# Value columns of two head pairs projected token-major in one group and convolved along tokens by shifted reads, in a gated-DeltaNet / mLSTM layer on Trainium2

## The chip, the cores and the metric

The kernel runs on one core of a Trainium2 chip. The metric is the device time of one execution in microseconds. The core has TensorE (PE in the profile; its weight loads are PEld), VectorE (DVE), ScalarE (ACT), GpSimd (POOL) and SyncE (SP), whose queue issues nearly all DMAs of this kernel.

## The reference

One decoder layer on 256 tokens of width 2048, with two branches, a gated DeltaNet (32 value heads in 16 pairs that share a query and a key head) and an mLSTM. All is float32. Cut to what matters here:

```python
h = rms_norm(x, norm_pre_w) * (1.0 + scale[:, None]) + shift[:, None]
proj = h @ w_in                                   # 16 groups of 512 columns for the pairs, and others
qkv = causal_conv_silu(gdn_qkv, gdn_conv_w)       # 4 taps along the tokens, per channel, then silu
q_a, k_a, v_a = jnp.split(qkv, [GDN_QK_WIDTH, 2 * GDN_QK_WIDTH], axis=-1)
q_a, k_a = l2_normalize(q_a) * 128 ** -0.5, l2_normalize(k_a)       # per head, shared by two value heads
o_a = gated_delta_rule(q_a, k_a, v_a, g_log, beta)                  # needs inverse of unit-lower matrices
o_a = rms_norm(o_a, gdn_norm_w) * silu(gdn_z)
y_a = o_a @ w_proj_gdn
# ... mLSTM branch gives y_b ...
merged = sigmoid(gate_a) * y_a + sigmoid(gate_b) * y_b
return x + gate * rms_norm(merged @ w_out, norm_post_w)
```

The convolution mixes a channel's value at token t with those at t-1, t-2 and t-3, each with its own weight per channel.

## The kernel before

**Precision.** Every large product takes float32 data as a rounded part and a remainder (`hi`, `lo`) and adds three products: hi·hi, hi·lo, lo·hi. Weights are split on the fly: a unit of weights (128x2048) is loaded by SP, and for each of its two pieces of 1024 columns ScalarE writes the rounded part (`whi`, line 173) and VectorE subtracts (`wlo`, line 177). Each has four buffers, the raw weights three. In the first part of the kernel, GpSimd does some of the subtractions.

**The stream.** `Stream.run` goes through all pieces in one order. It prepares up to four pieces ahead of the one that TensorE uses, issues the matmuls of a piece, then calls `side.step()`. A step so is one piece. All other work (convolutions, scores, block inverse, second stage, outputs) is written as generators that the `Side` object advances by one `yield` per step, in order of rank; `wait(n)` yields n times. `side.debt` is a planner's estimate of VectorE time that is booked and not yet worked off (1.6 us per step): the block inverse issues its next operation only when the debt leaves room.

**Two orientations.** `add_proj_t` projects channel-major: the weights are the stationary operand, the tokens (both halves of h side by side, 512 columns) move; per 128 rows of the contraction there are two matmuls of 512 columns (line 639) and two of 256 (line 643) for 256 output channels. `add_proj_n` projects token-major: h is stationary, 512 weight columns move, three matmuls of 512 columns for each block of 128 tokens (line 244). In both cases a piece is four such blocks.

**A period.** The DeltaNet runs in eight periods (`gdn_period(zg)`) of two head pairs. A pair's 512 columns are a query, a key and two value heads. Before the change a period is: channel-major pair 0 (8 pieces: first the half with query and key, then the half with two value heads), token-major output gate (`add_z`, 8 pieces), channel-major pair 1 (8 pieces), so 24 steps. For each half `conv_half` copies one part of the two sums on ScalarE (line 684), adds the other on VectorE (688), makes the first tap on ScalarE (691), three taps for each of two channel blocks on VectorE (697) and a Silu (705).

**Scores and values.** `gdn_stage1(p, ...)` forms the pair's score matrices (`psa`, `psb`, lines 761 to 766) when its convolutions are done, and transposes the four 128x128 blocks of values to token-major (`psv`, line 771), which ScalarE copies into `rr` scaled by the key norm (line 812). `block_rows` writes diagonal blocks of the scores to DRAM, `base_inverse` (after the second pair of the period) reads them back in another layout, inverts 32x32 blocks on VectorE, and writes and reads the result again (`ud`, `ug`, `xd`, `xcmp`). `gdn_stage2` starts at the earliest 31 steps after the second pair's scores; it puts the inverse together and applies it to `rr` (lines 960 to 989), then norms, gates and writes the heads to DRAM (`o_dr`).

**What sets the order.** Every engine executes its queue in program order, so an instruction that waits holds up those behind it; SP's queue holds weight loads and the transfers of the side work alike. The conv taps of the DeltaNet lie channel on partition in `gcv` (128x256, loaded by `late_consts`). Buffers of the pool `yp` (tags `ya`, `yhi`, `ylo`) serve `conv_half` here and the output projections later.

Of the kernel before, what the change touches and what calls it, by code (L numbers as in the profile page):

```python
# [7 lines left out]
F32 = mybir.dt.float32  # L8
F32R = mybir.dt.float32r
# [6 lines left out]
P = 128  # L16
# [102 lines left out]
def hybrid_layer_kernel(  # L119
# [153 lines left out]
    gate_row_dr = dr.tile([1, D], F32, name="gate_row_dr")  # L273
    START = [40 + g for g in range(8)] + [33, 37, 34, 38, 35, 39]
# [260 lines left out]
    def gates(ps):  # L535
# [52 lines left out]
        SP.dma_start(rows[32:40], mm_[64:72])  # L588
        yield from wait(3)
# [6 lines left out]
        V.tensor_scalar(ngt, tt[:, :, 0:32], -1.0, None, op0=ALU.mult)  # L596

# [28 lines left out]
    def add_proj_t(g, first, after, extra=None):  # L626

        w = w_in[g].rearrange("p (k n) -> p k n", k=KC)
        st_ = {}
        for hf in range(2):  # L630
            for t in range(2):
# [20 lines left out]
                stream.add(w[:, t * 8:(t + 1) * 8, hf * S:(hf + 1) * S], prep_w, use, after=done if t else None)  # L652
# [3 lines left out]
    def add_proj_n(g, after, extra=None):  # L656

        st_ = {}
        for t in range(4):
# [9 lines left out]
            stream.add(w_in[g][:, t * 2048:(t + 1) * 2048], prep_w, use, after=  # L669
# [4 lines left out]
    def conv_half(ps, taps, dst, hf, add=1, late=0, home=0, whole=False):  # L674
# [4 lines left out]
        elif home:  # L679
            ab = [bp.tile([P, S], F32, name="ab", tag=t, bufs=1) for t in ("p2", "tmp")]  # L680
        else:
            ab = [yp.tile([P, S], F32, name="ab", tag=("ya", ("yhi", "ylo")[i])[hf], bufs=3 - hf) for i in range(2)]
# [23 lines left out]

    def gdn_qk(ps, taps, qs, r, late):

        yield from conv_half(ps, taps, qs, 0, 1, late)
        qh = bp.tile([P, 2, S], F32R, name="qh", tag="qh", bufs=1)  # L710
        A.copy(qh, qs[:, 0:2])
        r.update(qh=qh)
# [29 lines left out]
    def gdn_taps(p):  # L742
        return lambda n, j: late_c["gcv"][:, (p * 4 + n) * 4 + j:(p * 4 + n) * 4 + j + 1]

    def gdn_stage1(p, ps, qs, pr, res):

        z = p % 2
        yield from conv_half(ps, gdn_taps(p), qs, 1, *((1, 0) if z else (3, 1)))
        qh = pr["qh"]
        side.debt += 0.7  # L750
        ql = bp.tile([P, 2, S], F32R, name="ql", tag="ql", bufs=1)
        V.tensor_tensor(ql, qs[:, 0:2], qh.bitcast(F32), op=ALU.subtract)
        yield
        gb = decay_rows(2 * p)
# [4 lines left out]
        yield from banks(3)  # L759
# [5 lines left out]
        for m in range(2):  # L765
            T.transpose(psb[:, 256 + m * P:256 + (m + 1) * P], qs[:, 0, m * P:(m + 1) * P], ident)
# [790 lines left out]
```

## Time and profile before

| | us |
|---|---|
| three runs: median (lowest to highest) | 1570.83 (1570.33 to 1573.07) |
| the profiled execution | 1570.67 |
| its span, first to last instruction | 1568.9 |
| mean granted TensorE clock | 0.998 |
| PE, DVE, ACT, POOL busy | 1555.8, 1166.0, 967.5, 261.5 |
| bytes moved by DMA | 372.22 MB, mean 237 GB/s |

The profile shows one execution. Busy times add up the time in which an engine had an instruction running. Matmuls are pipelined and their ends are modelled, so two neighbours overlap in the trace; how fast they follow one another is read from their starts. Rows of groups read: line, engine, operation, output and inputs, shapes, count | busy us, mean ns of one | idle time just before them and what ended it. Rows of the timeline read: start us, duration us, engine, line, operation, count of merged instructions. Rows of windows read: start:end, length, busy us and count for PE, PEld, DVE, ACT, POOL, then the granted clock, the share of DMA engines in use, and GB/s.

The eight periods lie between about 330 and 950 us; the mLSTM part, the output projections and the merge follow.

### The profile page before, as it was taken

To read this page: it belongs to the slowest core of one execution; us is meant where nothing else is said; L and a number is where in the kernel's file an instruction comes from. 1 tells how busy PE (TensorE), PEld (TensorE's weight loads), DVE (VectorE), ACT (ScalarE), POOL (GpSimd) and SP (SyncE) were. 2 spreads that over 40 slices of the span, in tenths; PEclk is the share of its full clock that TensorE was granted. 3 is DMA by queue.
4 is the path that set the end of the run, shared out by engine and by line. 5 is a ranking of instruction groups with operands and counts; after the bars stand their busy time and mean duration, and the time that the engine had idled before them with its cause. 6 is when DMAs were issued, how large, how long until landed. Compare 5 with 4: busy or idle time off the path is not lost.

```text
span 1568.9 us, 23204 instructions
## 1 busy us (share of the span) xinstructions
PE 1555.8 (99%) x8574; PEld 1308.5 (83%) x8574; DVE 1166.0 (74%) x1901; ACT 967.5 (62%) x1629; POOL 261.5 (17%) x212
## 2 busy tenths in 40 slices
PE   8999999999999999999999999999999999999997
PEld 5888888888888888888888888888888888888886
DVE  6785556765789898989898988776868866756654
ACT  7754446765666676767676777766566554544443
POOL 5787771000000010101010101000000000100100
PEclk9999999999999999999999999999999999999999
DMA  9998775975565656565656565657779877766573
GB/s 379 403 387 328 274 282 196 287 251 194 171 209 174 194 166 201 172 200 173 200 173 200 173 200 179 194 166 250 274 271 343 312 268 290 287 237 243 211 268 108
DMA packets 167739, 372.22 MB, mean 237 GB/s; under 512 B 26021, under 2 KB 127797, under 8 KB 140105
## 3 DMA queue, kind: packets, MB, share of 16 engines
q1 hardware_dynamic: 167240, 370.13, 68.2%
q8 instruction: 67, 1.10, 0.3%
q10 hardware_dynamic: 290, 0.53, 0.1%
q14 instruction: 46, 0.38, 0.1%
q0 software_dynamic: 96, 0.09, 0.0%
HBM read 354.40 MB, written 16.31 MB: 236 GB/s over the span
## 4 chain that ended last, share of the span: by engine, by line
PE 83%; issue 13%; DMA 2%; POOL 1%; ACT 1%; DVE 0%; SPq 0%; DVEq 0%; POOLq 0%; ACTq 0%
PE pn L244 38%; PE pt L639 19%; PE pt L643 9%; PE py L244 8%; POOL mg L1347 1%; DMA raw<-in_dram 1%; PE psa L244 1%; PE csil L314 0%; PE po L989 0%; PE po L988 0%; PE pc L978 0%; PE pb L968 0%; PE pa L960 0%; PE po L986 0%; PE pt L1028 0%
## 5 line engine op out<-in xcount | busy, mean ns | idle before, releaser
L177 DVE TENSOR_TENSOR wlo<-raw,whi 128x1024 fp32r<-128x1024 f32 (+1 forms) x455 | 558.8, 1236 | 221.6 <-ACT whi L173 220.5
L173 ACT CAST whi<-raw 128x1024 fp32r<-128x1024 f32 x508 | 523.9, 1046 | 269.4 <-PE pn L244 138.0
L244 PE MATMUL pn<-whi,h 128*128 128x512 f32 x1792 | 563.8, 392 | 1.2 <-ACT part L488 0.5
L639 PE MATMUL pt<-h,whi 128*128 128x512 f32 x1280 | 407.9, 400 | 0.0
L244 PEld LDWEIGHTS pn<-whi,h 128*128 128x128 f32 x1792 | 336.3, 188 | 72.3 <-ACT h L173 1.1
L244 PE MATMUL pn<-wlo,h 128*128 128x512 f32 x896 | 348.8, 389 | 0.0
L643 PEld LDWEIGHTS pt<-h,wlo 128*128 128x128 f32 x1280 | 240.4, 188 | 56.6
L643 PE MATMUL pt<-h,wlo 128*128 128x256 f32 x1280 | 251.9, 278 | 0.0
L639 PEld LDWEIGHTS pt<-h,whi 128*128 128x128 f32 x1280 | 195.5, 189 | 1.9
L244 PEld LDWEIGHTS pn<-wlo,h 128*128 128x128 f32 x896 | 168.3, 188 | 33.6
L177 POOL TENSOR_TENSOR wlo<-raw,whi 128x1024 fp32r<-128x1024 f32 (+1 forms) x67 | 146.5, 2199 | 47.3 <-ACT whi L173 41.6
L244 PE MATMUL py<-whi,yhi 128*128 128x512 f32 x384 | 150.6, 392 | 0.0
L244 PE MATMUL py<-whi,ylo 128*128 128x512 f32 x384 | 149.6, 390 | 0.0
L244 PE MATMUL py<-wlo,yhi 128*128 128x512 f32 x384 | 149.4, 389 | 0.0
L173 ACT CAST yhi<-ya 128x512 fp32r<-128x512 f32 x48 | 29.9, 623 | 127.6 <-PE py L244 124.3
L486 DVE TENSOR_TENSOR part<-pn,part 128x512 f32<-128x512 f32 x112 | 73.8, 686 | 45.1 <-PE pn L244 44.9
L730 POOL TENSOR_SCALAR_AFFINE_SELECT dd<-gb 128x256 f32<-128x256 f32 x40 | 33.9, 870 | 435.4 <-DMA gb<-rows 398.9
L177 DVE TENSOR_TENSOR ylo<-ya,yhi 128x512 fp32r<-128x512 f32 x48 | 33.2, 691 | 75.3 <-ACT yhi L173 71.8
L244 PEld LDWEIGHTS py<-whi,yhi 128*128 128x128 f32 x384 | 72.1, 188 | 15.3
L244 PEld LDWEIGHTS py<-whi,ylo 128*128 128x128 f32 x384 | 72.1, 188 | 15.1
L244 PEld LDWEIGHTS py<-wlo,yhi 128*128 128x128 f32 x384 | 72.1, 188 | 14.9
L697 DVE SCALAR_TENSOR_TENSOR qs<-ab,gcv,qs 128x255 f32<-128x255 f32 (+2 forms) x192 | 81.0, 477 | 0.0
(264 smaller groups left out, 1602.8 us busy)
## 6 DMA issues: line engine op xcount, KB each, us to landing
raw<-in_dram SPq DMA_DIRECT2D x259, 1024.0 KB
ar<-in_dram SPq DMA_DIRECT2D x31, 1024.0 KB
raw<-in_dram SPq DMA_DIRECT2D x16, 512.0 KB
ya<-o_dr SPq DMA_DIRECT2D x32, 256.0 KB
gate_dr<-part SPq DMA_DIRECT2D x11, 512.0 KB
gb<-rows SPq DMA_DIRECT2D x20, 256.0 KB
raw<-in_dram SPq DMA_DIRECT2D x6, 768.0 KB
ug<-ud SPq DMA_DIRECT2D x32, 128.0 KB
```

What stands on the lines that cost most here:

```text
L173: A.copy(hi, src)
L177: eng.tensor_tensor(lo, src, hi.bitcast(F32), op=ALU.subtract)
L244: T.matmul(ps, l, r, start=start and i == 0, stop=stop and i == 2, skip_group_check=True)
L486: V.tensor_tensor(part[g][:, b], ps[b], part[g][:, b], op=ALU.add)
L639: T.matmul(ps, hi[:, o:o + P], h2[:, k].rearrange("p a s -> p (a s)"), start=k == 0, stop=k == KC - 1, skip_group_check=True)
L643: T.matmul(ps[:, 0:S], lo[:, o:o + P], h_hi[:, k], start=False, stop=k == KC - 1, skip_group_check=True)
L697: V.scalar_tensor_tensor(dst[:, n, sh:], ab[i][:, 0:S - sh], taps(n, 3 - sh), dst[:, n, sh:], op0=ALU.mult, op1=ALU.add)
L730: G.affine_select(dd[:, :, blk * S:blk * S + P], gb[:, :, blk * P:(blk + 1) * P], pattern=[[0, 2], [1, P]], compare_op=ALU.is_ge, fill=-1e ...
L1347: G.tensor_tensor(mcols(b, hf, cg), mcols(b, hf, cg), s_, op=ALU.add)
```

## The change

A period becomes: query and key of both pairs channel-major (8 pieces: pair 0's, then pair 1's), the values of both pairs (4 heads, 512 columns) token-major in one group (8 pieces), the output gate (8 pieces). The transposes of values fall away, since the values come out token-major.

Token-major, the convolution runs along partitions. So `gdn_values` copies the sums to `rr`, waits 11 steps, writes them to a DRAM buffer `vd` (three rows of zeros stand ahead of the tokens), and reads them back shifted by one, two and three rows. The taps, now needed along the free dimension and equal on all partitions, are transposed once at the end of `gates`, written to `conv_dr` and read with a broadcast over 128 partitions in each period. GpSimd multiplies two of the shifted copies with their taps and adds them; VectorE does the other two and the remaining sums; ScalarE applies Silu and the key norm's scale. The second stage waits in its generator until `rr` is ready.

`gdn_stage1` convolves only query and key; both pairs share one tile `qs`. In `base_inverse` two waits become the same for all periods. `conv_half` takes its buffers from the tag `ylo` throughout, where it isn't in the late mLSTM pairs.

```diff
     def load_w(src):
-        for s_ in src if isinstance(src, tuple) else (src,):
+        for i, s_ in enumerate(src if isinstance(src, tuple) else (src,)):
+            if isinstance(src, tuple) and len(s_.shape) == 3:
+                SP.dma_start(raw.rearrange("p (k g c) -> p k g c", k=4, g=2)[:, :, i], s_)
+                continue
...
+    conv_dr = dr.tile([NPAIR, 4, 4, P], F32, name="conv_dr")
+    vd = dr.tile([S + 3, 512], F32, name="vd")
...
+        for z in range(2):
+            SP.dma_start(vd[0:3, z * S:(z + 1) * S], zz[0:3])
...
+        gct, gcp = t_("gct"), t_("gcp")
+        G.tensor_copy(gcp.rearrange("c (p t n) -> c p t n", n=4, t=4),
+                      late_c["gcv"].rearrange("c (p n t) -> c p t n", n=4, t=4))
+        yield from wait(2)
+        tc_ = gtile("tc")
+        for b in range(2):
+            T.transpose(tc_[:, b * P:(b + 1) * P], gcp[:, b * P:(b + 1) * P], ident)
+        A.copy(gct, tc_[:, 0:S])
+        yield from wait(2)
+        for b in range(2):
+            SP.dma_start(conv_dr[8 * b:8 * b + 8].rearrange("p t n c -> (p t n) c"), gct[:, b * P:(b + 1) * P])
...
     def add_proj_t(g, first, after, extra=None):
-        w = w_in[g].rearrange("p (k n) -> p k n", k=KC)
         for hf in range(2):
+            w = w_in[g[hf] if isinstance(g, tuple) else g].rearrange("p (k n) -> p k n", k=KC)
+            c0 = 0 if isinstance(g, tuple) else hf * S
...
     def add_proj_n(g, after, extra=None):
...
+            if isinstance(g, tuple):
+                src = tuple(w_in[i].rearrange("p (k n) -> p k n", k=KC)[:, 4 * t:4 * t + 4, S:2 * S] for i in g)
...
-    def gdn_stage1(p, ps, qs, pr, res):
+    def gdn_stage1(p, ps, qs, res):
         z = p % 2
-        yield from conv_half(ps, gdn_taps(p), qs, 1, *((1, 0) if z else (3, 1)))
-        qh = pr["qh"]
+        yield from conv_half(ps, gdn_taps(p // 2), qs, z)
+        qz = qs[:, 2 * z:2 * z + 2]
+        qh = bp.tile([P, 2, S], F32R, name="qh", tag="qh", bufs=1)
+        A.copy(qh, qz)
+        gb = decay_rows(2 * p)
+        yield from wait(1 + z)
         side.debt += 0.7
         ql = bp.tile([P, 2, S], F32R, name="ql", tag="ql", bufs=1)
...
-        psv = gtile("psv", True)
-        side.debt -= 1.6
-        for blk in range(2):
-            for h in range(2):
-                T.transpose(psv[:, (blk * 2 + h) * P:(blk * 2 + h + 1) * P],
-                            qs[:, 2 + h, blk * P:(blk + 1) * P], ident)
+        side.debt -= 1.2
...
-        for blk in range(2):
-            A.activation(res["rr"][:, blk, z], psv[:, blk * S:(blk + 1) * S], AF.Copy, scale=sk[:, blk:blk + 1])
-        gfree(psv)
+    def gdn_values(zg, ps, res):
+        rr = bp.tile([P, 2, 2, S], F32, name="rr", tag="rr")
+        for b in range(2):
+            A.copy(rr[:, b].rearrange("p z c -> p (z c)"), ps[b])
+        yield from wait(11)
+        SP.dma_start(vd[3:].rearrange("(b t) c -> t b c", b=2), rr.rearrange("p b z c -> p b (z c)"))
+
+        def tap_rows(w, z, j):
+            SP.dma_start(w, conv_dr[2 * zg + z, j:j + w.shape[1], 2:4].rearrange("t n c -> t (n c)").unsqueeze(0)
+                         .broadcast_to(list(w.shape)))
+
+        def shifted(z, j):
+            v = yp.tile([P, 2, S], F32, name=f"v{j}", tag="yhi" if z and j > 1 else "ya", bufs=2 if z and j > 1 else 3)
+            SP.dma_start(v, vd[3 - j:3 - j + S, z * S:(z + 1) * S].rearrange("(b t) c -> t b c", b=2))
+            return v
+        ws = {}
+
+        def tap(e, z, v, j):
+            side.debt += 0.7 if e is V else 0.0
+            e.tensor_tensor(v, v, ws[z, 3 - j].unsqueeze(1).broadcast_to([P, 2, S]), op=ALU.mult)
+
+        def plus(e, a, b):
+            side.debt += 0.7 if e is V else 0.0
+            e.tensor_tensor(a, a, b, op=ALU.add)
+        yield from wait(2)
+        vs = [[rr[:, :, z], None, None, None] for z in range(2)]
+        for z, j in ((0, 1), (0, 2), (0, 3), (1, 2), (1, 3)):
+            yield
+            vs[z][j] = shifted(z, j)
+        yield
+        w = bp.tile([P, 4, S], F32, name="cw", tag="qs")
+        tap_rows(w, 0, 0)
+        ws.update({(0, j): w[:, j] for j in range(4)})
+        yield from wait(3)
+        for i in range(2):
+            w = yp.tile([P, 2, S], F32, name="cw", tag="ylo", bufs=2)
+            tap_rows(w, 1, 2 * i)
+            ws.update({(1, 2 * i + j): w[:, j] for j in range(2)})
+            yield
+        yield
+        for z in range(2):
+            v = vs[z]
+            tap(G, z, v[2], 2)
+            tap(G, z, v[3], 3)
+            plus(G, v[2], v[3])
+            tap(V, z, v[0], 0)
+            yield
+            tap(V, z, v[1], 1)
+            yield
+            plus(V, v[0], v[1])
+            if z == 0:
+                vs[1][1] = shifted(1, 1)
+            yield
+            plus(V, v[0], v[2])
+            yield
+        A.activation(rr, rr, AF.Silu)
+        yield
+        for z in range(2):
+            for b in range(2):
+                A.activation(rr[:, b, z], rr[:, b, z], AF.Copy, scale=res["sk", z][:, b:b + 1])
+        res["rr"] = rr
...
     def base_inverse(zg, res, zr):
-        yield from wait(2 * (zg // 7))
+        yield from wait(2)
...
-        yield from wait(5 - 2 * (zg // 7))
+        yield from wait(3)
...
     def gdn_stage2(zg, res, zr):
+        while "rr" not in res:
+            yield
         rr = res["rr"].rearrange("p b z (h d) -> p b (z h d)", h=2)
...
     def gdn_period(zg):
         res = {}
-        def pair(z, after):
-            p, pr = 2 * zg + z, {}
-            add_proj_t(p, lambda ps, qs: gdn_qk(ps, gdn_taps(p), qs, pr, 2 if z else 5),
-                       lambda ps, qs: side.add(after(ps, qs, pr)))
-        pair(0, lambda ps, qs, pr: gdn_stage1(2 * zg, ps, qs, pr, res))
+        pair = 2 * zg, 2 * zg + 1
+        add_proj_t(pair, lambda ps, qs: gdn_stage1(pair[0], ps, qs, res),
+                   lambda ps, qs: side.add(period_tail(zg, ps, qs, res, zrs[zg])))
+        add_proj_n(pair, lambda ps: side.add(gdn_values(zg, ps, res)))
         add_z(zg)
-        pair(1, lambda ps, qs, pr: period_tail(zg, ps, qs, pr, res, zrs[zg]))
```

More of the change, by code (lines that the diff above doesn't have):

```diff
@@ L651, in done @@
                         after(st_["ps"], st_["dst"])
-                stream.add(w[:, t * 8:(t + 1) * 8, hf * S:(hf + 1) * S], prep_w, use, after=done if t else None)
+                stream.add(w[:, t * 8:(t + 1) * 8, c0:c0 + S], prep_w, use, after=done if t else None)
                 if extra:
@@ L668, in use @@
                             hi[:, o:o + 512], lo[:, o:o + 512], k == 0, k == KC - 1)
-            stream.add(w_in[g][:, t * 2048:(t + 1) * 2048], prep_w, use, after=
+            if isinstance(g, tuple):
+                src = tuple(w_in[i].rearrange("p (k n) -> p k n", k=KC)[:, 4 * t:4 * t + 4, S:2 * S] for i in g)
+            else:
+                src = w_in[g][:, t * 2048:(t + 1) * 2048]
+            stream.add(src, prep_w, use, after=
                        (lambda: after(st_["ps"])) if t == 3 else None)
@@ L681, in conv_half @@
         else:
-            ab = [yp.tile([P, S], F32, name="ab", tag=("ya", ("yhi", "ylo")[i])[hf], bufs=3 - hf) for i in range(2)]
+            pair = yp.tile([P, 2, S], F32, name="ab", tag="ylo", bufs=2)
+            ab = [pair[:, i] for i in range(2)]
         for i in range(2):
@@ L705, in conv_half @@
         A.activation(dst[:, 2 * hf:2 * hf + 2], dst[:, 2 * hf:2 * hf + 2], AF.Silu)
[L707 to L712, printed above, removed]
     o_dr = dr.tile([32, P, S], F32, name="o_dr")
@@ L740, in decay_exp, with gdn_taps, taps @@
             A.activation(dd[:, h, S:384], dd[:, h, S:384], AF.Exp, bias=b22[:, h:h + 1])
[L742 to L749 removed]
+    def gdn_taps(zg):
+        def taps(n, j):
+            c = ((2 * zg + n // 2) * 4 + n % 2) * 4 + j
+            return late_c["gcv"][:, c:c + 1]
+        return taps
+    def gdn_stage1(p, ps, qs, res):
+        z = p % 2
+        yield from conv_half(ps, gdn_taps(p // 2), qs, z)
[4 more added lines that the diff above has]
+        yield from wait(1 + z)
         side.debt += 0.7
         ql = bp.tile([P, 2, S], F32R, name="ql", tag="ql", bufs=1)
[L752 to L754 removed]
+        V.tensor_tensor(ql, qz, qh.bitcast(F32), op=ALU.subtract)
         dd = decay_mask(gb)
@@ L758, in gdn_stage1 @@
         yield from wait(2)
-        yield from banks(3)
+        yield from banks(2)
         res["t"] = side.t
@@ L1033, in gdn_stage2, with period_tail @@
             SP.dma_start(o_dr[4 * zg + 2 * z:4 * zg + 2 * z + 2].rearrange("h d t -> d h t"), oT)
-    def period_tail(zg, ps, qs, pr, res, zr):
-        yield from gdn_stage1(2 * zg + 1, ps, qs, pr, res)
+    def period_tail(zg, ps, qs, res, zr):
+        yield from gdn_stage1(2 * zg + 1, ps, qs, res)
         yield
```

5 lines of the change are left out of this document (2 added, 3 removed).

## The prediction

> **What bounds the kernel now.** First comes the page: its list of engines, and its chain of work that ended last.
>
> ```profile
> PE 1555.8 (99%) x8574; PEld 1308.5 (83%) x8574; DVE 1166.0 (74%) x1901; ACT 967.5 (62%) x1629; POOL 261.5 (17%) x212
> PE 83%; issue 13%; DMA 2%; POOL 1%; ACT 1%; DVE 0%; SPq 0%; DVEq 0%; POOLq 0%; ACTq 0%
> ```
>
> TensorE is busy nearly throughout, and the chain is TensorE's own. Since its ends are modelled, I ask next who waits for whom (times: in total, how often, longest), and what one 80 us window in the middle of the eight head periods holds (engine busy times, granted clock, DMA share, GB/s).
>
> ```profile
> DVE wlo L177 <- ACT whi L173: 220.5, 209, 5.9
> ACT whi L173 <- PE pn L244: 138.0, 103, 2.1
> ACT whi L173 <- PE pt L639: 65.3, 53, 2.6
> ACT whi L173 <- DMA raw<-in_dram: 17.5, 8, 3.6
> 660.00:740.00 80.00, 80.00 (x550) 69.18 (x549) 70.08 (x150) 57.76 (x117) 8.08 (x10) 1.00 0.60 185
> ```
>
> The waits run one way: VectorE waits for ScalarE's rounded weights, and ScalarE waits for TensorE to give the weight buffers back. No wait of TensorE for either is in the list above these. In the window TensorE has no idle microsecond at full clock (1.00), VectorE has 9.9 us left, ScalarE 22. So **what TensorE no longer does is gained, as long as the others stay inside their spare time.**
>
> The length of a period comes from the gate activation, two per period:
>
> ```profile
> L1047 ACT ACTIVATE sz<-pn x16: 582/588/599, 378.4 to 914.8; 128x512 f32<-128x512 f32 x16
> ```
>
> First to last, less the 0.6 us between the two of one period, over 7: 76.5 us. A period is 24 steps (weight pieces), so 3.19 us a step.
>
> **TensorE's sum.** The timeline of TensorE, one value-like block (three matmuls of 512 columns, line 244) and one channel-major block (two of 512, two of 256, lines 639 and 643), each by its first and last start in an undisturbed stretch; then the transposes that the change drops.
>
> ```profile
> 579.97 0.62 PE L244 MATMUL pn<-whi,h 128*128 128x512 f32 x2
> ...
> 587.45 0.62 PE L244 MATMUL pn<-whi,h 128*128 128x512 f32 x2
> ...
> 613.47 0.38 PE L766 MATMUL psb<-con,qs 128*128 128x128 f32 x2
> 613.69 0.60 PE L771 MATMUL psv<-con,qs 128*128 128x128 f32 x4
> 614.05 0.71 PE L639 MATMUL pt<-h,whi 128*128 128x512 f32 x2
> ...
> 633.23 0.63 PE L639 MATMUL pt<-h,whi 128*128 128x512 f32 x2
> ...
> 638.10 0.63 PE L639 MATMUL pt<-h,whi 128*128 128x512 f32 x2
> ```
>
> The columns streamed are equal: both blocks hold 1536. But 11 token-major blocks took 7.48 us, 0.680 each, and 7 channel-major blocks took 4.87 us, 0.696 each. A step has four blocks of either kind (2.72 and 2.78 us). Per period the value halves, 8 steps or 32 blocks, change kind: 32 x 0.0157 = 0.50 us, and over 8 periods **4.0 us**. Its lower bound is nothing (equal columns); I take the measured difference.
>
> The four transposes of values go, once per pair. The next matmul began 0.36 us after the first of them; 16 x 0.36 = **5.8 us**. The bounds are nothing, if weight loads fill the gap, and 16 x 0.60 = 9.6 us, if the whole row counted. I take the distance of starts, since that is how matmuls follow one another here.
>
> Added on TensorE are two transposes of the tap table, once: at 0.11 us (0.22 between the psb row and the psv row, for two) with a switch around them, 0.3 us. The sum is -4.0 - 5.8 + 0.3 = **-9.5 us**.
>
> **What the others get, per period.** Grouped rows, shapes apart (busy, mean ns):
>
> ```profile
> L688 DVE TENSOR_TENSOR ab<-pt,ab 128x256 f32<-128x256 f32 x80 | 29.9, 416 | 0.0
> L697 DVE SCALAR_TENSOR_TENSOR qs<-ab,gcv,qs 128x255 f32<-128x255 f32 x64 | 27.9, 478 | 0.0
> L177 DVE TENSOR_TENSOR ylo<-ya,yhi 128x512 fp32r<-128x512 f32 x48 | 33.2, 691 | 75.3 <-ACT yhi L173 71.8 <-PE pnum L1112 3.5
> L684 ACT COPY ab<-pt 128x256 f32<-128x256 f32 x80 | 25.7, 377 | 8.9 <-PE pt L643 8.9
> L691 ACT ACTIVATE qs<-ab,gcv 128x256 f32<-128x256 f32 x64 | 29.1, 506 | 2.4 <-DVE ab L688 2.4
> L705 ACT ACTIVATE qs<-qs 128x512 f32<-128x512 f32 x32 | 20.2, 632 | 7.6 <-DVE qs L697 7.2
> L812 ACT ACTIVATE rr<-psv,sk 128x256 f32<-128x256 f32 x32 | 13.4, 470 | 0.0
> L1000 ACT COPY on<-po 128x512 f32<-128x512 f32 x16 | 9.3, 578 | 0.0
> L703 ACT ACTIVATE qs<-qs 128x1024 f32<-128x1024 f32 x4 | 4.2, 1060 | 0.0
> ```
>
> VectorE loses two value convolutions, each 2 adds (0.416) and 6 multiply-adds (0.478): 2 x 3.70 = 7.4 us. It gains 4 tap products and 4 sums of 128x512, at 0.691 from the nearest row of that shape with two SBUF inputs: 5.5 us. Net -1.9 us.
>
> ScalarE loses 4 copies (0.377), 4 first taps (0.506), 2 Silus (0.632) and 4 scalings (0.470), 6.7 us; it gains 2 copies (0.578), one Silu of 1024 (1.06) and 4 scalings (0.506), 4.2 us. Net -2.4 us. Neither reaches the end; they only widen the cover.
>
> GpSimd gains 4 products and 2 sums of 128x512. Its nearest row, and what VectorE did beside it:
>
> ```profile
> L1347 POOL TENSOR_TENSOR mg<-mg,gs x8: 1285/2046/2295, 1343.0 to 1477.1; 128x512 f32<-128x512 f32 x8
> 1342.98 7.54 POOL L1347 TENSOR_TENSOR mg<-mg,gs 128x512 f32<-128x512 f32 x4 [119.57 <-DMA raw<-in_dram]
> 1343.28 2.07 DVE L177 TENSOR_TENSOR wlo<-raw,whi 128x1024 fp32r<-128x1024 f32 x1
> 1347.07 4.53 DVE L177 TENSOR_TENSOR wlo<-raw,whi 128x1024 fp32r<-128x1024 f32 x2
> 1352.13 1.21 DVE L177 TENSOR_TENSOR wlo<-raw,whi 128x1024 fp32r<-128x1024 f32 x1
> ```
>
> Four such sums took 7.54 us, 1.9 each (the quickest 1.285), and the weight subtractions beside them took 2.07 and 2.27 us where 1.21 is usual: (2.07 - 1.21) + (4.53 - 2.42) = 3.0 us of VectorE lost to four, 0.75 to each. So the two engines hinder one another. Six a period cost VectorE between nothing (they miss its two-input work) and 6 x 1.285 = 7.7 us (it stands still for each); I take 6 x 0.75 = 4.5 us. With the -1.9, VectorE is 2.6 us a period fuller (5.8 at worst), against 9.9 spare in 80: TensorE doesn't feel it on average. *The Trainium skill (SBUF — State Buffer, SBUF: two separate sides) says that a GpSimd instruction reading SBUF and a VectorE instruction with two SBUF inputs exclude one another for their whole length; the rows agree in kind, VectorE's delay being about 0.75 us per GpSimd instruction.* In place, the cover is this: the weight buffers are four deep, so a piece's preparation starts when TensorE has three pieces (8.2 us) in hand, and it takes 1.05 + 1.22 us of ScalarE and VectorE. VectorE may be some 5.9 us late before TensorE waits.
>
> **Waits that are added.** VectorE's third sum waits for GpSimd's three instructions, at 1.9 us 5.7 us, issued three steps (8.2 us) earlier: nothing; behind it in VectorE's queue stand weight subtractions, for which TensorE waits. If GpSimd began 3 us late, the wait would be 0.5 us. On SP, the first shifted read waits for the landing of the written values, three steps after the write; behind it stand weight loads. ScalarE's Silu of the values and stage 2's first product wait for these sums; stage 2 comes by my count of yields 3 to 4 steps after them and would only slide, TensorE going on with projections. The second pair's scores now run at step 17 of a period instead of 32, and their low halves are ready two steps ahead (5.4 us) instead of three: no cost as long as VectorE is less than about 4 us behind.
>
> **Transfers.** Per period are added the write of the values (0.52 MB), six shifted reads of 0.26 MB, and taps for 128 partitions of 1.05 MB: 3.1 MB. SP issues 14 more DMAs (four of them since each value unit loads from two groups).
>
> ```profile
> 660.00:663.00 3.00, 3.00 (x15) 2.49 (x14) 3.00 (x4) 2.14 (x4) 0.18 (x1) 1.00 0.98 320
> L832 SPq DMA_DIRECT2D ug<-ud x32: 605/610/1027, 440.7 to 993.0; - x32
> SPq L169 <- DVE wlo L177: 646.1, 164, 8.9
> ```
>
> At full share 320 GB/s moved (first row), so 3.1 MB are 9.8 us of 76.5, and the share goes from 0.60 to some 0.73. Issue at 0.61 us (the second row) is 8.5 us of a queue that mostly waits for VectorE to release weight buffers (third row). A weight unit (two pieces) is loaded four pieces, 11 us, before its first use and takes 1.05 MB / 320 = 3.3 us: 7.6 us of cover, and behind it the 5.9 us above. I take nothing; the upper end is all 9.8 us of traffic in front of weight loads, minus 7.6 of cover, 2.2 us a period, 18 us in all.
>
> **The rivals.**
>
> *A: TensorE's sum (forecast).* The profiled execution took 1570.67 us (span 1568.9), the median of the runs is 1570.83. 1570.7 - 9.5 = **1561.2**. With the bounds above of its two terms, 1557.4 (9.6 for the transposes) to 1565.2 (no gain from token-major blocks). Chance 0.60.
>
> *B: part of it comes back*, as short waits at the scores, the late sums or loads: 0.5 us to 1 us a period, 4 to 8 us, so 1565 to 1569. For it speaks that both pairs' scores, the values and the block inverse now crowd into steps 4 to 24. Against it: VectorE was not fully used in the window. Chance 0.16; most of it still is faster.
>
> *C: no change.* The added 3.1 MB delay weight loads by about 1.2 us a period beyond their cover, 9.5 us in all: 1571. For it: at 0.98 share a 3 us stretch is already full. Against it: the mean 0.60, and ScalarE waited for loads only 17.5 us in the whole run. Chance 0.11.
>
> *D: slower, by the exclusion of GpSimd and VectorE.* Place: steps 17 to 24 of each period, where VectorE has 8 weight subtractions (9.8 us), the 5.5 us of taps, the second pair's scores (about 3.6 by the debts that the code books for them) and the inverse's pieces that fill its spare time by the planner's debt; GpSimd's blocking is in no debt. If VectorE is already 5.9 us late there, each blocked microsecond becomes TensorE's: 4.5 us x 8 = 36, hence 1570.7 - 9.5 + 36 = 1597; 7.7 us each give 1623. It decides from the point where blocking and backlog pass 5.9 us; the gain is gone at 1.2 us a period beyond it. *By that rule of the Trainium skill taken literally, every one of the six would block for its whole length, the worst of these; the trace shows 0.75 instead.* Against it: those steps have 8 x 2.75 = 22 us, plus the scores. Chance 0.13.
>
> That the change doesn't do what it says can hardly be: the dropped transposes and the kind of block are visible in the program. Left out would be only the gain from blocks (in A's upper bound).
>
> **How the numbers follow.** 0.2%, 3.1 us, is about what a measurement of this kernel tells from no change. Faster than that is A and most of B, 0.60 + 0.14 = 0.74; the same is C and the rest of B, 0.13; slower is D, 0.13. The range holds A, B and the nearer part of C: 1557 to 1570, with about 0.8 of the chance.
>
> **What would show it.** Right: the period between gate activations shrinks from 76.5 to 75.3 us; blocks stay at 0.680 and 0.696; no wait of TensorE for VectorE or DMA enters the list of waits. Wrong: TensorE idle in steps 17 to 24 with weight subtractions above 2 us beside GpSimd (D); ScalarE waiting for weight loads by over 1 us a period (C); gaps before the scores (B). What would break the forecast at once is a TensorE below 100% in the middle windows.

## The result and the profile after

| | before | after |
|---|---|---|
| median (lowest to highest, six runs each), us | 1570.63 (1570.33 to 1574.62) | 1599.27 (1596.36 to 1603.04) |
| profiled execution, us | 1570.67 | 1603.04 |
| its span, us | 1568.9 | 1601.2 |
| mean granted TensorE clock | 0.998 | 0.990 |

The changed kernel takes 1.0178 times as long as the kernel before (95% interval 1.016 to 1.0196). The forecast was 1561.2 us, faster; the time came out on the other side and far outside the range, within 3 us of rival D's 1597. The profiled execution is the slowest of the six, so its rows show the loss at its largest.

The page of the changed kernel, busy times (us, share of the span, instructions):

```profile
PE 1562.8 (98%) x8256; PEld 1300.0 (81%) x8256; DVE 1202.4 (75%) x1837; ACT 952.9 (60%) x1574; POOL 342.0 (21%) x261
```

and the shares of its chain that ended last:

```profile
PE 64%; issue 14%; DVE 13%; DMA 5%; POOL 2%; SPq 1%; ACT 1%; DVEq 0%; POOLq 0%; ACTq 0%
```

TensorE has fallen from 99% to 98% busy, VectorE stands in the chain with 13%, and GpSimd has 80.5 us more than before's 261.5. VectorE was to lose 1.9 us a period; it gained 36.4 us in the run (1202.4 against 1166.0).

The waits of the changed kernel (total, times, longest, in us):

```profile
PE pn L247 <- DVE wlo L180: 15.3, 9, 2.3
ACT whi L176 <- DMA raw<-in_dram: 42.6, 15, 5.3
```

The first was not in the list before: TensorE now waits for weight remainders (`wlo`) of VectorE. The waits for weight loads rose from 17.5 to 42.6 us; the second experiment tells whether that costs anything.

One period in the changed kernel. VectorE's timeline (start us, duration us, line, operation, count):

```profile
696.97 1.14 DVE L1098 SCALAR_TENSOR_TENSOR on<-on,so,sz 128x128 f32<-128x128 f32 x4
...
700.54 2.47 DVE L1098 SCALAR_TENSOR_TENSOR on<-on,so,sz 128x128 f32<-128x128 f32 x4
702.94 2.31 DVE L180 TENSOR_TENSOR wlo<-raw,whi 128x1024 fp32r<-128x1024 f32 x1
705.17 1.78 DVE L849 TENSOR_TENSOR rr<-rr,cw 128x512 f32<-128x512 f32 x1
706.87 1.21 DVE L180 TENSOR_TENSOR wlo<-raw,whi 128x1024 fp32r<-128x1024 f32 x1
708.01 0.68 DVE L849 TENSOR_TENSOR v<-v,cw 128x512 f32<-128x512 f32 x1
...
710.20 2.59 DVE L950 COPY y<-ycmp 32x256 f32<-32x256 f32 x2
712.83 2.25 DVE L180 TENSOR_TENSOR wlo<-raw,whi 128x1024 fp32r<-128x1024 f32 x1
```

GpSimd's, in the same stretch:

```profile
701.45 2.71 POOL L849 TENSOR_TENSOR v<-v,cw 128x512 f32<-128x512 f32 x2
704.24 2.15 POOL L853 TENSOR_TENSOR v<-v,v 128x512 f32<-128x512 f32 x1
...
710.07 2.58 POOL L849 TENSOR_TENSOR v<-v,cw 128x512 f32<-128x512 f32 x2
712.73 1.27 POOL L853 TENSOR_TENSOR v<-v,v 128x512 f32<-128x512 f32 x1
```

And TensorE's, where the release stands in brackets:

```profile
708.02 0.39 PE L247 MATMUL pn<-wlo,h 128*128 128x512 f32 x1
...
708.70 0.39 PE L247 MATMUL pn<-wlo,h 128*128 128x512 f32 x1
...
712.67 0.48 PE L247 MATMUL pn<-whi,h 128*128 128x512 f32 x1
715.14 0.50 PE L247 MATMUL pn<-wlo,h 128*128 128x512 f32 x1 [1.98 <-DVE wlo L180]
...
716.25 0.63 PE L247 MATMUL pn<-wlo,h 128*128 128x512 f32 x1
...
717.53 0.63 PE L247 MATMUL pn<-wlo,h 128*128 128x512 f32 x1
```

Read the three side by side. GpSimd works from 701.45 to 706.39 and from 710.07 to 714.00. What VectorE runs outside these stretches has its usual length (gate products 1.14 at 696.97, subtraction 1.21 at 706.87, tap 0.68 at 708.01). Inside them it is longer: gate products 2.47, subtraction 2.31, tap 1.78, copies 2.59 (0.58 without GpSimd, in the second experiment), subtraction 2.25. That is 1.33 + 1.10 + 1.10 + 2.01 + 1.04 = 6.6 us in the period, 1.1 us for each of GpSimd's six operations.

The first burst takes 1.33 + 1.10 + 1.10 = 3.5 us from VectorE, and TensorE does not wait yet. But VectorE has no idle row between the bursts, so it carries the delay along. Behind the second burst TensorE waits: the subtraction that starts at 712.83 ends at 715.08, and TensorE stands from 713.16 to 715.14. Without the second burst's 2.01 + 1.04 us it would have ended at 712.03, 1.1 us before TensorE needed it, and without the first one's 3.5 us also in time. By this estimate from the rows it takes both.

Then a second price, the clock. The windows of the changed kernel around that wait (start:end, length, busy us of PE, PEld, DVE, ACT and POOL, granted clock, DMA share, GB/s):

```profile
712.00:715.00 3.00, 1.15 (x10) 0.84 (x8) 2.97 (x2) 2.20 (x3) 1.92 (x2) 1.00 0.00 0
715.00:718.00 3.00, 2.86 (x8) 2.24 (x9) 3.00 (x5) 0.00 (x0) 0.00 (x0) 0.59 0.56 181
718.00:721.00 3.00, 3.00 (x13) 2.41 (x12) 3.00 (x6) 1.05 (x1) 0.00 (x0) 0.84 0.82 264
```

After 2 us without work the granted clock is 0.59 and then 0.84: 3 x 0.41 + 3 x 0.16 = 1.7 us of TensorE's speed. The blocks, 0.68 us from `wlo` to `wlo` at 708, are 1.28 us at 716. At this place a wait of 2 us so costs 3.7. The Trainium skill (TensorE: Matmul & The Clock Gate, Part 1: The HAM clock gate) ties the low clock to an idle window of about 3.4 us; here a wait of 1.98 us brought it.

Over the whole kernel the clock counts for less than that. The six executions took 1603.0 and 1601.5 us at a mean clock of 0.990, 1598.1 at 0.993, 1597.8 and 1600.4 at 0.995, and 1596.4 at 0.998, which is the clock of the kernel before. In that last execution the change still costs 26 us.

### The profile page after: what moved, and what is told of

It reads as the page before. It is cut to its first block, busy times and chain, and to the rows that moved or that the text cites. A ratio compares the mean times of both kernels' runs of the same rounds, so it can differ in the third digit from the quotient of the medians.

```text
span 1601.2 us, 22616 instructions
## 1 busy us (share of the span) xinstructions
PE 1562.8 (98%) x8256; PEld 1300.0 (81%) x8256; DVE 1202.4 (75%) x1837; ACT 952.9 (60%) x1574; POOL 342.0 (21%) x261
## 4 chain that ended last, share of the span: by engine, by line
PE 64%; issue 14%; DVE 13%; DMA 5%; POOL 2%; SPq 1%; ACT 1%; DVEq 0%; POOLq 0%; ACTq 0%
PE pn L247 38%; PE pt L658 8%; PE py L247 8%; DVE wlo L180 5%; PE pt L662 4%; DMA raw<-in_dram 2%; DMA ug<-ud 1%; DVE on L1098 1%; DVE y L950 1%; POOL mg L1424 1%; DVE rr L849 1%; DVE tmp L928 1%; DVE au L816 1%; DMA xs<-in_dram 1%; DVE xx L932 1%
## 5 line engine op out<-in xcount | busy, mean ns | idle before, releaser
L247 PE MATMUL pn<-whi,h 128*128 128x512 f32 x2304 | 736.4, 396 | 1.4 <-ACT part L493 0.7
L180 DVE TENSOR_TENSOR wlo<-raw,whi 128x1024 fp32r<-128x1024 f32 (+1 forms) x455 | 571.5, 1264 | 192.9 <-ACT whi L176 191.4
L176 ACT CAST whi<-raw 128x1024 fp32r<-128x1024 f32 x508 | 523.0, 1044 | 289.9 <-PE pn L247 155.0
L247 PEld LDWEIGHTS pn<-whi,h 128*128 128x128 f32 x2304 | 437.4, 190 | 93.0 <-ACT part L493 1.1
L247 PE MATMUL pn<-wlo,h 128*128 128x512 f32 x1152 | 454.2, 394 | 15.3 <-DVE wlo L180 15.3
L247 PEld LDWEIGHTS pn<-wlo,h 128*128 128x128 f32 x1152 | 219.2, 190 | 62.9 <-DVE wlo L180 19.5
L658 PE MATMUL pt<-h,whi 128*128 128x512 f32 x768 | 247.3, 403 | 0.0
L662 PEld LDWEIGHTS pt<-h,wlo 128*128 128x128 f32 x768 | 144.9, 189 | 34.0
L662 PE MATMUL pt<-h,wlo 128*128 128x256 f32 x768 | 151.9, 279 | 0.0
L747 POOL TENSOR_SCALAR_AFFINE_SELECT dd<-gb 128x256 f32<-128x256 f32 x40 | 34.9, 895 | 467.5 <-DVE xx L934 203.9
L658 PEld LDWEIGHTS pt<-h,whi 128*128 128x128 f32 x768 | 118.7, 190 | 2.5
L176 ACT CAST yhi<-ya 128x512 fp32r<-128x512 f32 x48 | 29.9, 622 | 128.2 <-PE py L247 117.0
L247 PE MATMUL pw<-whi,m 128*128 128x512 f32 x256 | 80.0, 391 | 0.0
```

The source lines that it names most:

```text
L176: A.copy(hi, src)
L180: eng.tensor_tensor(lo, src, hi.bitcast(F32), op=ALU.subtract)
L247: T.matmul(ps, l, r, start=start and i == 0, stop=stop and i == 2, skip_group_check=True)
L658: T.matmul(ps, hi[:, o:o + P], h2[:, k].rearrange("p a s -> p (a s)"), start=k == 0, stop=k == KC - 1, skip_group_check=True)
L662: T.matmul(ps[:, 0:S], lo[:, o:o + P], h_hi[:, k], start=False, stop=k == KC - 1, skip_group_check=True)
L747: G.affine_select(dd[:, :, blk * S:blk * S + P], gb[:, :, blk * P:(blk + 1) * P], pattern=[[0, 2], [1, P]], compare_op=ALU.is_ge, fill=-1e ...
```

## The experiments

Theory D: GpSimd's six operations hold VectorE up, and that alone turns the gain into a loss. Rivals: the added transfers (C), the order of the second pair's scores (B), or a gain of TensorE that was never there (A wrong). Medians are compared with the kernel before in the same session, 1570.6 to 1571.0 us.

### TensorE's sum by itself

The convolution of the values is left out of the changed kernel:

```diff
-        yield from wait(11)
-        SP.dma_start(vd[3:].rearrange(...), rr.rearrange(...))
...
-            plus(V, v[0], v[2])
-            yield
+        yield from wait(33)
         A.activation(rr, rr, AF.Silu)
```

> Leaves out the convolution of the values: no write and shifted reads, no taps, no products and sums; Silu and the scale stay at their steps. Exclusion theory (GpSimd's six instructions a period hold VectorE up, TensorE then waits, and its clock drops): none of that is left, so TensorE's sum stands, 1561 to 1564 us, a period of 75.3 us. Crowding theory (both pairs' scores and the inverse now meet in the same steps): the scores still do, so 1566 to 1580. Transfer theory (3.1 MB more a period delay weight loads): 1561 to 1564.

Measured: 1559.53 us (1559.48 to 1561.14), ratio 0.9932 (0.991 to 0.9955). TensorE's part is worth 11.0 us; the forecast had 9.5, between bounds of 5.5 and 13.3. The gain was real, and it is TensorE's own: TensorE is 1544.6 us busy here against 1555.8 before. The time lies 1.5 us under what was expected. Both pairs' scores run at their new steps in this kernel too, so their order (B) costs nothing that shows.

### Without GpSimd's six operations

The transfers and VectorE's eight operations per period stay; GpSimd's four products and two sums are left out:

```diff
-            tap(G, z, v[2], 2)
-            tap(G, z, v[3], 3)
-            plus(G, v[2], v[3])
             tap(V, z, v[0], 0)
```

> Leaves out GpSimd's two products and one sum per pair (the taps of the two oldest tokens); all transfers and all of VectorE's work stay. Exclusion: 1561 to 1567, weight subtractions at 1.2 us throughout. Crowding: about 1590, since VectorE's own work is the same. Transfers: about 1595, since every byte still moves.

Measured: 1562.11 us (1561.78 to 1563.95), ratio 0.9949 (0.9927 to 0.9972). So transfers and VectorE's eight operations cost 2.6 us together, and GpSimd's six cost 1599.3 - 1562.1 = 37.2 us. Its page, busy times:

```profile
PE 1545.2 (99%) x8256; PEld 1291.3 (83%) x8256; DVE 1153.9 (74%) x1837; ACT 953.6 (61%) x1574; POOL 267.1 (17%) x213
```

and one of its waits:

```profile
ACT whi L176 <- DMA raw<-in_dram: 41.7, 19, 5.5
```

ScalarE waits for weight loads as long as in the changed kernel (41.7 against 42.6 us), and the time is 37 us shorter: these waits are covered, and C falls. Leaving the six out also takes away VectorE's wait for GpSimd's sums, but no such wait stands in the changed kernel's list. The difference of the two profiled spans, 1601.2 - 1560.0 = 41.2 us, splits into 17.6 us more TensorE busy time for the same 8256 matmuls (the granted clock is 0.990 against 0.999, which makes some 14 of them: 1601.2 x 0.010 less 1560.0 x 0.001) and 23.6 us more idle time, of which 15.3 are the waits for `wlo`. VectorE is 48.5 us busier in the changed kernel though it has the same 1837 instructions: 1.0 us for each of GpSimd's 48 operations.

Where VectorE's time went shows in the grouped rows, first of the changed kernel:

```profile
L1098 DVE SCALAR_TENSOR_TENSOR on<-on,so,sz 128x128 f32<-128x128 f32 x64 | 32.8, 572 | 1.5 <-POOL so L243 1.5
L950 DVE COPY y<-ycmp 32x256 f32<-32x256 f32 x16 | 16.6, 1036 | 0.4
L849 DVE TENSOR_TENSOR rr<-rr,cw 128x512 f32<-128x512 f32 x16 | 18.5, 1159 | 0.0
```

and then of the kernel without the six:

```profile
L1095 DVE SCALAR_TENSOR_TENSOR on<-on,so,sz 128x128 f32<-128x128 f32 x64 | 20.2, 375 | 0.1
L947 DVE COPY y<-ycmp 32x256 f32<-32x256 f32 x16 | 4.5, 283 | 0.4
L849 DVE TENSOR_TENSOR rr<-rr,cw 128x512 f32<-128x512 f32 x16 | 10.9, 682 | 0.0
```

The gate products lose 12.6 us, the inverse's copies 12.1, the first tap 7.6.

The kernel without the six also shows how much cover there was. These are ScalarE, VectorE and TensorE at the place that in the changed kernel lies at 710 to 715: two roundings, the copies of `y` with the subtraction of the first rounding behind them, and the matmul with `wlo` behind the eight transposes, which there waited 1.98 us.

```profile
691.98 2.00 ACT L176 CAST whi<-raw 128x1024 fp32r<-128x1024 f32 x2
693.76 0.58 DVE L947 COPY y<-ycmp 32x256 f32<-32x256 f32 x2
694.37 1.23 DVE L180 TENSOR_TENSOR wlo<-raw,whi 128x1024 fp32r<-128x1024 f32 x1
697.67 1.04 PE L1104 MATMUL pt<-con,on 128*128 128x128 f32 x8
...
698.77 0.40 PE L247 MATMUL pn<-wlo,h 128*128 128x512 f32 x1
```

The subtraction ends at 695.60, 3.2 us before TensorE uses it. Its rounding began 6.8 us before that use, when ScalarE had done four other copies, and VectorE came to it 1.3 us after the rounding's end (at 693.0), behind the copies of `y`. So neither engine began at once, and the cover was 3.2 us.

### The six on VectorE

```diff
-            tap(G, z, v[2], 2)
-            tap(G, z, v[3], 3)
-            plus(G, v[2], v[3])
+            tap(V, z, v[2], 2)
             tap(V, z, v[0], 0)
             yield
+            tap(V, z, v[3], 3)
             tap(V, z, v[1], 1)
             yield
+            plus(V, v[2], v[3])
             plus(V, v[0], v[1])
```

> GpSimd's four products and two sums a period move to VectorE, with their debt booked; the result is the reference's. VectorE gets 6 x 0.69 = 4.1 us of work and loses the 6.6 us of delay counted in one period. Exclusion: faster than the changed kernel, 1565 to 1582. Crowding: slower than it, 1600 to 1615. Transfers: no change, about 1598.

Measured: 1567.8 us (1566.34 to 1571.02, eight runs), ratio 0.9987 (0.9976 to 0.9998). The same six operations cost 5.7 us on VectorE and 37.2 us on GpSimd. Its page, busy times:

```profile
PE 1547.1 (99%) x8256; PEld 1291.0 (82%) x8256; DVE 1181.9 (75%) x1885; ACT 953.4 (61%) x1574; POOL 268.5 (17%) x213
```

its window from 660 to 740 us (columns as in the windows above):

```profile
660.00:740.00 80.00, 80.00 (x516) 68.16 (x515) 73.31 (x152) 56.74 (x110) 7.39 (x9) 1.00 0.73 227
```

and the same window of the changed kernel:

```profile
660.00:740.00 80.00, 78.02 (x497) 66.05 (x496) 69.45 (x127) 52.14 (x102) 16.02 (x15) 0.98 0.71 214
```

VectorE, doing the six itself, is busy 1181.9 us; with GpSimd doing them it is busy 1202.4. Handing them over costs it 20.5 us more than keeping them. TensorE is full in the first window (80.00) and not in the second (78.02).

### GpSimd's work in the kernel before

To take the change away and keep only the suspect, the kernel before gets six products of 128x512 a period on GpSimd, into a tile that nobody reads:

```diff
+    def idle_products():
+        yield
+        t = yp.tile([P, 2, S], F32, name="idle", tag="ya", bufs=3).rearrange("p a b -> p (a b)")
+        for i in range(2):
+            for _ in range(3):
+                G.tensor_tensor(t, con, con, op=ALU.mult)
+            yield from wait(4)
...
+            side.add(idle_products())
         add_proj_n(16 + zg, z_after)
```

> The kernel before with six products of 128x512 with two SBUF inputs on GpSimd in each period, into a tile that nobody reads. VectorE should lose 4.5 to 7.7 us a period in the exclusion theory, where it had 9.9 us spare: its weight subtractions beside them above 1.8 us, the time 1571 to 1585. Crowding and transfers alone: 1571, and no subtraction longer.

Measured: 1589.8 us (1589.35 and 1590.24), ratio 1.0121 (1.0092 to 1.015). Work that nobody waits for makes the old kernel 19.2 us slower, more than the 1585 that was expected at most. VectorE is 16.6 us busier (1182.6 against 1166.0) with the same instructions. VectorE and GpSimd in one timeline:

```profile
698.85 1.22 DVE L177 TENSOR_TENSOR wlo<-raw,whi 128x1024 fp32r<-128x1024 f32 x1
...
700.92 1.10 DVE L857 SCALAR_TENSOR_TENSOR xx<-xx,nsu 128x4 f32<-128x4 f32 x1
...
700.96 9.08 POOL L1048 TENSOR_TENSOR idle<-con 128x512 f32<-128x512 f32 x6
...
703.99 0.35 DVE L855 TENSOR_REDUCE xx<-tmp 128x10 f32<-128x190 f32 x1
...
707.06 2.08 DVE L177 TENSOR_TENSOR wlo<-raw,whi 128x1024 fp32r<-128x1024 f32 x1
```

and a wait of TensorE that the kernel before does not have:

```profile
PE pt L643 <- DVE wlo L177: 8.4, 5, 2.1
```

Beside the products the inverse's sums (line 857) take 1.10, 0.56, 0.51 and 0.49 us, where each takes 0.23 in the kernel before, and the second subtraction takes 2.08: 2.6 us are lost. TensorE then waited 2.05 us for this subtraction, so without the loss it would, by this estimate, have been in time. In the kernel before 6.8 us lie between the same two subtractions (690.84 and 697.60), but there VectorE stands idle for the last 0.20 of them, until the rounding is ready; it is not late.

One other wait grew: ScalarE's for the decay masks `dd`, which GpSimd makes (36.1 us against 14.2). In the period shown a DMA set the start of the masks, not the products. What this wait adds was not measured apart.

### Telling the planner

If the loss comes from blocked time that the planner doesn't know of, booking it should help:

```diff
-            side.debt += 0.7 if e is V else 0.0
+            side.debt += 0.7 if e is V else 0.8
```

(in `tap` and in `plus`, in the changed kernel)

> The changed kernel; each GpSimd product and sum now books 0.8 us of VectorE's time in the planner's debt (4.8 us a period), so the inverse issues less beside them. If TensorE waits because unbooked blocking comes on top of a VectorE that the planner has already filled: 1575 to 1590, against 1599. If the blocking alone is enough, whatever else VectorE is given: 1597 to 1602.

Measured: 1602.84 us (two runs), ratio 1.0203 (1.0183 to 1.0224): no gain, and 0.8 us above the upper range. Booked debt only holds back the block inverse's operations, and in the changed kernel the bursts meet gate products, subtractions, taps and copies, none of which the planner can hold back. In this run's trace the same five of them took 2.47, 2.31, 1.78, 2.60 and 2.25 us, as without the booking.

### Products with one input

The same as the fourth, with `G.tensor_scalar` in place of `G.tensor_tensor`:

```diff
-                G.tensor_tensor(t, con, con, op=ALU.mult)
+                G.tensor_scalar(t, con, 2.0, None, op0=ALU.mult)
```

> The kernel before with six GpSimd instructions a period as in the run with products, but with one input each (a product with a constant), into a tile that nobody reads. If an instruction's second input is what excludes VectorE: 1571 to 1573. If any GpSimd instruction that reads SBUF does: 1582 to 1590, as with two inputs (1589.8).

Measured: 1580.66 us, ratio 1.0062 (1.0042 to 1.0082), 9.8 us slower than before, about half of the two-input products' 19.2 and between the two ranges that were expected. One input holds VectorE up too, and less (8.7 us busier than before, against 16.6), although each of them took GpSimd a little longer (median 1492 ns against 1394).

### Where in the period it falls

Two more runs place the same work elsewhere. In the kernel before, six products and a half one are made to wait for the end of the block inverse:

```diff
         res.update(xcmp=xcmp, ycmp=ycmp)
+        t = yp.tile([P, 2, S], F32, name="idle", tag="ya", bufs=3).rearrange("p a b -> p (a b)")
+        G.tensor_tensor(t[:, 0:S], ycmp.rearrange("p m i -> p (m i)"), con[:, 0:S], op=ALU.mult)
+        for _ in range(6):
+            G.tensor_tensor(t, con, con, op=ALU.mult)
```

> The kernel before with the same six GpSimd products of two inputs a period (and a half one ahead of them, which reads the inverse's transposed blocks and so holds them back), now behind the inverse's end, where VectorE waits 1.5 and 1.9 us for weights within 8 us in the trace of before. If the place decides (blocking hurts where VectorE is booked full): 1571 to 1577. If blocking costs the same anywhere: 1587 to 1592, as beside the inverse (1589.8).

Measured: 1579.06 us, ratio 1.0054 (1.0033 to 1.0074): 8.1 us slower than the kernel before in its session, instead of 19.2, with more GpSimd work; the time lies between the two ranges, nearer to the lower. Its gate activations (the last two times are the starts of the first and the last):

```profile
L1051 ACT ACTIVATE sz<-pn x16: 585/589/600, 378.1 to 916.1; 128x512 f32<-128x512 f32 x16
```

a burst of GpSimd, with VectorE beside it:

```profile
674.95 7.67 POOL L878 TENSOR_TENSOR idle<-con 128x512 f32<-128x512 f32 x6
678.12 3.61 DVE L697 SCALAR_TENSOR_TENSOR qs<-ab,gcv,qs 128x254 f32<-128x254 f32 x3
```

and the window behind the last period's burst, which runs from 1052 to 1061:

```profile
1060.00:1100.00 40.00, 36.83 (x232) 32.03 (x232) 26.94 (x39) 23.07 (x53) 2.00 (x3) 0.96 0.65 224
```

with TensorE's wait in it:

```profile
1065.99 0.63 PE L1145 MATMUL mpt<-con,hn 128*128 128x128 f32 x4 [3.17 <-DVE x L925]
```

Between the activations lie 538.0 us (before: 916.1 in place of 914.8 at the end, 536.4 in all), so seven periods lost 1.6 us. VectorE is held up even more than in the fourth experiment (28.2 us busier than before, there 16.6; three multiply-adds take 3.61 us here, usually 1.26), but where it has room TensorE doesn't feel it. Most of the loss comes behind the last period's burst: 3.2 us of idle TensorE, which waits for VectorE, and a clock of 0.96 (1.6 us) between 1060 and 1100; the kernel before has TensorE full there (40.00). Beside that burst four gate products took 4.18 us, usually 1.13, and four products of the mLSTM 3.91, usually 0.48 each. This burst met a place without room.

In the changed kernel, products and sums come four steps later, behind the block inverse's copies:

```diff
-        yield
+        yield from wait(5)
         for z in range(2):
             v = vs[z]
             tap(G, z, v[2], 2)
...
         while "rr" not in res:
             yield
+        yield
```

> The changed kernel with all of the values' products and sums four steps later, GpSimd's too (with one step more before stage 2's first product). If the place decides: the blocking leaves the steps with the scores and the inverse's copies and meets a VectorE that waits for weights 2 of 3 us: 1570 to 1585. If not: 1597 to 1605.

Measured: 1610.59 us, ratio 1.0254 (1.0234 to 1.0275). A miss of both ranges: later was worse by 11 us, not better, although VectorE lost less (31.6 us busier than without the six, 48.5 in the changed kernel). The second stage waits for these values and slid with them, so GpSimd met the gate products again, and these in turn TensorE's transposes. Four gate products undisturbed and beside GpSimd, in its timeline:

```profile
712.39 1.13 DVE L1099 SCALAR_TENSOR_TENSOR on<-on,so,sz 128x128 f32<-128x128 f32 x4
715.67 5.27 DVE L1099 SCALAR_TENSOR_TENSOR on<-on,so,sz 128x128 f32<-128x128 f32 x4
```

and the largest wait of TensorE in it:

```profile
PE pt L1108 <- DVE on L1099: 15.5, 19, 1.0
```

The next is for the scores' low halves (`PE psa` for `ql`, 8.4 us).

### Versions that go on from the six on VectorE

Four runs tried to win more than that one. First, the inverse's copies move from VectorE to ScalarE:

```diff
-                V.tensor_copy(y0[c, :, c], ycmp[c])
+                A.copy(y0[c, :, c], ycmp[c])
...
-            V.tensor_scalar(x0[64:96, sides[i], 96:128], fours(psx[1], (64, 0)[i]), -1.0, None, op0=ALU.mult)
+            A.activation(x0[64:96, sides[i], 96:128], fours(psx[1], (64, 0)[i]), AF.Copy, scale=-1.0)
```

> As the run with all products and sums on VectorE (1567.8), and four small copies a period that VectorE makes in the inverse and stage 2 (1.15 us) go to ScalarE. If VectorE's load in the crowded steps is what is left between 1567.8 and the run without GpSimd's work (1562.1): 1564 to 1567. If it isn't: 1567 to 1570.

Measured: 1585.84 us (1584.68 to 1587.14), ratio 1.0093 (1.0076 to 1.011). A miss of both ranges, and 18 us above the third experiment. ScalarE's timeline in this kernel:

```profile
705.51 0.41 ACT L950 COPY y<-ycmp 32x256 f32<-32x256 f32 x1 [3.68 <-DVE ycmp L945]
707.52 2.94 ACT L176 CAST whi<-raw 128x1024 fp32r<-128x1024 f32 x3
```

Over the run ScalarE waits 28.5 us for `ycmp` in eight waits, one a period. The copy needs a transpose that VectorE makes late. On VectorE it stood behind that transpose at no cost; on ScalarE it makes the engine stand for 3.68 us, and the weight roundings queued behind it, for which VectorE's subtractions and TensorE wait, come in a bunch of three.

The same with the values' operations two steps later (the expectation says three; the edit makes it two):

```diff
-        yield
+        yield from wait(3)
         for z in range(2):
             v = vs[z]
```

> As the run with the copies on ScalarE, and the products and sums of the values start three steps later, towards the steps in which VectorE waits for weights (2 us of 3 idle). Crowding of VectorE as the rest: 1562 to 1565. A later stage 2 that costs more than it spares: 1567 to 1575.

Measured: 1586.73 us, ratio 1.0101 (1.0084 to 1.0118), above both ranges and nothing gained; the wait for the transpose grew to 33.0 us. Then the third experiment with only the second of the two edits, the copy from PSUM, where TensorE's results stand:

```diff
-            V.tensor_scalar(x0[64:96, sides[i], 96:128], fours(psx[1], (64, 0)[i]), -1.0, None, op0=ALU.mult)
+            A.activation(x0[64:96, sides[i], 96:128], fours(psx[1], (64, 0)[i]), AF.Copy, scale=-1.0)
```

> All products and sums on VectorE, and of the four small copies only the two of stage 2 that read TensorE's result go to ScalarE; the two behind the transpose stay on VectorE. If the 18 us between the runs with and without those copies on ScalarE came from ScalarE standing behind VectorE's late transpose: 1565 to 1569. If from anything else in that edit: 1575 to 1587.

Measured: 1567.54 us (1566.49 to 1570.46, ten runs), ratio 0.9982 (0.9972 to 0.9991). So the 18 us were the copies of `ycmp`; the ones from PSUM cost and bring nothing that shows beside the third experiment's 1567.8. And the third experiment with only the two steps of delay:

```diff
-        yield
+        yield from wait(3)
         for z in range(2):
```

> All products and sums on VectorE, two steps later, nothing on ScalarE. VectorE's crowding as the rest of the loss: 1563 to 1567; stage 2 waiting for the values: 1568 to 1575.

Measured: 1569.92 us, ratio 0.9993 (0.9984 to 1.0002): no gain over 1567.8, and in the range for a second stage that waits for the values. Its trace has that wait (`PE pa` for `rr`, 4.3 us), which the third experiment's has not. The best version found here takes 1567.5 us and is 0.2% faster than the kernel before; of TensorE's 11.0 us, the transfers and the convolution on VectorE take back 2.6 + 5.7.

## Why the prediction was wrong

**TensorE's sum** was right: -9.5 us foretold, -11.0 measured with the convolution left out. In the changed kernel's trace the token-major blocks stand at 0.68 us wherever the clock is whole (708.02, 708.70). How the 11.0 divide between blocks and transposes was not measured.

**The transfers (C)** cost nothing to speak of: the DMA share rose to 0.71 (foretold: 0.73), loads came later (42 us of ScalarE's waits), and all of it together with VectorE's eight operations cost 2.6 us. The sign set for C, over 1 us a period of such waits, so came up without C being the cause. **Rival B** cost nothing that shows in the first two experiments. In the changed kernel it adds little (`PE psa` for `ql`, 2.3 us in three waits).

**The steps that failed** both belong to the exclusion of GpSimd and VectorE:

1. "Six a period cost VectorE between nothing … and 6 x 1.285 = 7.7 us …; I take 6 x 0.75 = 4.5 us." Measured in one period: 6.6 us; over the run 48.5 us for 48 operations, 1.0 each or 6.1 a period. The row that was taken, four sums beside weight subtractions, undersized it: there VectorE stood idle for 1.7 of GpSimd's 7.5 us (the first subtraction ends at 1345.35, the next starts at 1347.07), while in the changed kernel it has no idle row in the whole stretch shown. The rule cited from the Trainium skill (SBUF — State Buffer, SBUF: two separate sides) has one of the two blocked for the other's whole instruction; with the quickest length of 1.285 us that made the estimate of 7.7. The period shown lies nearer to it than to 4.5, the run's mean about midway.
2. "VectorE is 2.6 us a period fuller …, against 9.9 spare in 80: TensorE doesn't feel it on average", and in place "VectorE may be some 5.9 us late before TensorE waits." The average was no cover, because much of the spare time lies elsewhere in the period (the six products behind the inverse's end found it). In place the 5.9 took it that a rounding starts with 8.2 us in hand and that rounding and subtraction follow at once. The kernel without the six shows 6.8 us in hand, 1.3 us until VectorE comes to the subtraction, and 3.2 us of cover. Against a loss of 6.6 us that was too little: 1.0 us more came from a wait of VectorE for ScalarE just ahead (`[1.01 <-ACT whi L176]` at 690.41 in that kernel), which fell away. That leaves 2.4 us; TensorE waited 1.98. Already in the kernel before, the shortest distance in the eight periods from the end of a subtraction to its first use, with both counted in order, is 3.1 us (501.95 to 505.00).

**The clock** was not in the sum at all. Behind a wait of 2 us it took 1.7 us more at the place shown, but between the runs at a mean clock of 0.990 and the one at 0.998 lie 5 to 7 us only, of the 37. Why it adds up to so little was not tested.

**Rival D** named place, mechanism and nearly the price (1597 against 1599.3). In the period shown TensorE waits at the last piece but two, and beside GpSimd the subtractions take over 2 us, both signs that had been set for D. Its price was right partly by luck: it took a VectorE already 5.9 us late, so that 4.5 us a period of loss all became TensorE's. Measured were 6.1 us of loss, some of it covered, and a lower clock, and the price by the second experiment is 37.2 / 8 = 4.65 us a period. The chance of 0.13 was the mistake: it rested on a mean and on a cover that was never there.

**A check that was mis-set:** the period between gate activations was to shrink from 76.5 to 75.3 us. The row without the convolution, then without GpSimd, then of the changed kernel:

```profile
L1075 ACT ACTIVATE sz<-pn x16: 591/595/600, 403.1 to 937.9; 128x512 f32<-128x512 f32 x16
```

```profile
L1123 ACT ACTIVATE sz<-pn x16: 590/594/600, 403.3 to 940.0; 128x512 f32<-128x512 f32 x16
```

```profile
L1126 ACT ACTIVATE sz<-pn x16: 590/596/602, 402.7 to 974.3; 128x512 f32<-128x512 f32 x16
```

The first gives (937.9 - 403.1 - 0.6) / 7 = 76.3 us, though that kernel is 11 us faster than before: the output gate has moved to the end of the period, and the interval holds more work than it did, 48 of each of the second stage's products of 128x128 against 40, which is one period's more. Among the three, which have one order, it serves: 571.6 - 536.7 = 34.9 us of the 41.2 between the profiled spans arise between these activations.

## What to carry to other kernels

An elementwise operation handed from a busy VectorE to GpSimd can cost VectorE more than doing it: here 1.0 us of hold-up against 0.68 of work. Read the cover of a delay at the place where it falls, as the time from the end of a preparation to its first use in the trace, and not from the engine's mean load or from the number of buffers: here 3.2 us, where the mean promised 9.9 and the buffers 5.9. Before a copy moves to another engine, ask what it waits for and what stands behind it there.

## What the runs showed of the hardware

- VectorE is not held up by GpSimd in its two-input operations alone: the two copies of 32x256 took 2.59 us beside GpSimd and 0.58 without. A reduction with one input kept its 0.35 us in the middle of GpSimd's products (fourth experiment, 703.99), while the sums around it went from 0.23 to about 0.5 us. That section of the Trainium skill names such copies beside the two-input operations; the rows agree.
- GpSimd's products with one input hold VectorE up as well, at about half the cost in time (9.8 against 19.2 us).
- A pause of TensorE of 2 us was followed by 3 us at a granted clock of 0.59 and 3 us at 0.84.
